# Splitting weights in pairs of rows and summing conditioning 1024 columns at a time, in a two-layer trunk on one Trainium2 core

## The chip, the cores and the metric

The kernel runs on one core of one Trainium2 chip (trn2). The metric is the device time of one execution in microseconds (us); the kernel before took 1552.6 us, the median of 3 runs (1552.41 to 1552.89).

## What is computed

Two layers of a conditioned decoder trunk over 256 tokens of width 1024, in fp32. Per layer, with the vector c of conditioning:

```python
mod = silu(c) @ ada_w[l] + ada_b[l]                  # 1024 x 6144
sh1, sc1, gt1, sh2, sc2, gt2 = split(mod, 6)
h = rms_norm(x, norm1_g[l]) * (1 + sc1) + sh1
proj = h @ w_in[l]                                   # 1024 x 3524
ya = retention(...); yb = forgetting_attention(...); yc = latent_attention(...)
g  = sigmoid(h @ gate_w + gate_b)                    # 1024 x 3072
x += gt1 * ((g0 * (ya @ br0) + g1 * (yb @ br1) + g2 * (yc @ br2)) @ out_w)
h = rms_norm(x, norm2_g[l]) * (1 + sc2) + sh2
x += gt2 * moe(h)                                    # 32 experts, top 2 of one group of 8
```

The two attentions are softmax attentions with 4 heads each, over blocks of 128 queries. A last RMSNorm follows the second layer.

## The kernel before, in words

**Stages.** The program runs mixer 0 (about 0 to 345 us of the trace), MoE 0 (to 790), mixer 1 (to 1077) and MoE 1 (to the end). All weights come from HBM through one ring of 12 slots of 1 MB (`SLOTS`, L58; the DMAs are issued on SP at L139), in one planned order. A slot is given back when its weights have been used, and the next transfer of the plan starts then. For a MoE the ring grows to 20 slots, in memory that the mixer has left: two on the right side and three in `ar` while the mixer still runs, three on the left (`open_extra(l, "left", 3)`, L1204) once its output projection is done.

**Rows of weights.** A mixer's products are made of "rows": 128 x 512 (or 128 x 452) weights against all tokens. For fp32 precision a row is split into a high and a low fp32r part, and each product takes three matmuls (`mm3`). `split_w` (L244) splits one row: ACT casts it into the high part (L253), DVE subtracts that from the weights (L255). There are four buffers `ws`. `pump` (L240) splits until three rows lie ready; `next_w` calls it before it hands a row to the matmuls, and `gemm_tok`, `gemm_feat` and `out` call it again behind each row's matmuls, before they yield. A layer has 144 rows.

**What else runs beside the rows.** At each yield the driver takes one step of every live generator: an attention (`softmax_head`, L652: scores on PE, bias and maximum on DVE, exponential on ACT at L664, after two more steps the normalising on DVE at L669, then the transposes on PE at L188 and their copy on ACT at L675), retention, and the conditioning chain. Instructions of an engine are issued in the order in which this interleaving writes them.

**Conditioning.** `ada` (L485) multiplies silu(c) into `ada_w`. Most of it is summed on DVE, since c is one vector: `acc` gets a 128 x 512 multiply (L509) and then 128 x 512 multiply-adds (L511), four to a 1 MB chunk of four row blocks of 512 columns, one per step; a 32-column matmul sums `acc` over partitions at the end. The result is read with one DVE add of the bias (L529) and, where sums lie in several partition groups, ACT copies (L531). At the start of the program the first four parts go over PE instead, straight from the slots, and `space` (before L1564) puts two `warm` matmuls (L190) behind each of the first four chunks; their result is not used. `gs` turns the sums into the scale and shift that the first `head` (L959) needs to form `hr`, the split activations, and no row can be multiplied before that.

**Out.** `out` (L1167) multiplies the last 16 rows; behind the last row of each half of the columns `residual` (L588) adds the result to x (L592, L593 on DVE, the squares on ACT at L594).

Of the kernel before, what the change touches and what calls it, by code (L numbers as in the profile page):

```python
# [17 lines left out]
P = 128  # L18
# [3 lines left out]
DEPTH = 2  # L22
# [35 lines left out]
SLOTS = 12  # L58
# [107 lines left out]
class Trunk:  # L166
# [73 lines left out]
    def pump(self):  # L240
        while self.stream and len(self.splits) < len(self.ws) - 1:
            self.split_w()

    def split_w(self):  # L244
# [11 lines left out]
        self.splits.append((hi, lo))  # L256
# [12 lines left out]
    def setup(self, pool, psum):  # L269
# [30 lines left out]
        self.adab = t("adab", [64, 512])  # L300
# [11 lines left out]
    def open_split(self, l):  # L312
# [3 lines left out]
        self.ws = [t(f"ws{i}", [P, 2, 512]) for i in range(4)]  # L316
# [40 lines left out]
    def plan_mixer(self, l):  # L357
# [4 lines left out]
        def put_ada(n):  # L362
            for _ in range(min(n, len(adas))):
                l_, m, h = adas.popleft()
                add((l_, "ada", m, h), rows(a["ada_w"][l_, m, h], 4), [P, 4, 512])

        def cols(name, w, c0, n, split=True, halves=(0, 1)):
            for h in halves:
                key = (l, name, c0, h)
                add(key, rows(w[h], 4), [P, 4, n])  # L370
                if split:
                    stream.extend((key, i, n, i == 3) for i in range(4))
                    put_ada(min(len(adas) - ADA_TAIL, spread.get((l, name, c0), 0)))

        adas = deque((l, m, h) for m in ((0, 2, 1, 3) if l == 0 else ()) + tuple(range(4, 12)) for h in range(2))
        if l + 1 < DEPTH:
            adas.extend((l + 1, m, h) for m in range(4) for h in range(2))
# [15 lines left out]
        for br in (2, 1, 0):  # L393
            for h in range(2):
# [3 lines left out]
                stream.extend((key, i, 512, i == 3) for i in range(4))  # L398
# [86 lines left out]
    def ada(self, l, m0, ms, space, R, vec=()):  # L485

        nc, ps = self.nc, self.S[3]
        full, begun = [], set()  # L490
# [6 lines left out]
        for m in ms:  # L497
            for h in range(2):
                key = (l, "ada", m0 + m, h)
                while vec and self.ring.behind(key) < (0 if self.hurry else ADA_LAG):  # L500
                    yield
                slot, v = self.ring.take(key)
                end = m == ms[-1] and h == 1
                if m in vec:
                    acc = self.acc[:, len(full)]
                    for t in range(4):
                        c = self.cz[:, 4 * h + t, 23:24]
                        if h == 0 and t == 0:
                            nc.vector.tensor_scalar(acc, v[:, t, :], c, None, ALU.mult)  # L509
                        else:  # L510
                            nc.vector.scalar_tensor_tensor(acc, v[:, t, :], c, acc, ALU.mult, ALU.add)  # L511
                        if t < 3:
                            yield from space(-1)
                    if h:
                        full.append(m)
                        if len(full) == 2 or m + 1 not in vec:
                            for _ in range(ADA_DELAY):
                                yield
                            for i, k in enumerate(full):
                                add_up(i, 8, k, self.acc[:, i], end)  # L520
                            full = []
                else:
                    for t in range(4):
                        add_up(t, 4 * h + t, m, v[:, t, :], end)
                self.ring.give(slot)
                yield from space(2 * m + h)
# [7 lines left out]
        return R[:n], all(m in vec for m in ms)  # L534

    def picks(self, rows, r, n=1):

        R, vec = rows
        if vec:
            return self.ident[:R.shape[0], r:r + 66].rearrange("p (q x) -> p q x", q=2)[:, :, 0:2 * n:2]  # L540
        return self.sel[:R.shape[0], r:r + 2 * n].rearrange("p (v q) -> p q v", q=2)

    def gs(self, l, i, r, rows, rows1=None):
# [4 lines left out]
        sv, R = self.picks(rows, r, 2), rows[0]  # L548
        R1 = rows1[0] if rows1 else R
# [25 lines left out]
    def gate_rows(self, r, off, rows, banks=None):  # L575

        self.gtb = self.v(off, D)
        sv, R = self.picks(rows, r), rows[0]
# [23 lines left out]
    def gemm_tok(self, n, evac, js=range(8), pa=None):  # L602

        pa = pa or [self.bank("g") for _ in range(NT)]
        for j in js:
# [5 lines left out]
            self.pump()  # L611
# [5 lines left out]
    def gemm_feat(self, acts, evac, js=None, pa=None):  # L617
# [3 lines left out]
        for j in js or range(nk):  # L621
# [8 lines left out]
            self.pump()  # L630
# [21 lines left out]
    def softmax_head(self, i, h, scores, bias, val, yr):  # L652
# [15 lines left out]
        for k, s in enumerate(parts):  # L668
            nc.vector.tensor_scalar(s, s, rs[:, k:k + 1], None, ALU.mult)  # L669
# [289 lines left out]
    def head(self, l):  # L959
# [43 lines left out]
        def split(n):  # L1003
            for _ in range(n):
                self.split_w()

# [13 lines left out]
        split(l)  # L1020
# [4 lines left out]
        split(l)  # L1025

    def mixer(self, l):
# [17 lines left out]
        def chain():  # L1045
            self.rowsA = yield from self.ada(l, 4, range(6), space, self.R, range(6))
# [7 lines left out]
            self.rowsB = yield from self.ada(l, 10, range(2), lambda i: later(i + 1), self.v(A_RB, 512),  # L1054
                                             range(min(2, inline // 2)))
            if l + 1 < DEPTH:
                rows = yield from self.ada(l + 1, 0, range(4), lambda i: later(i + 5 if i >= 0 else -1), self.acc[:, 1],
                                           range((inline - 4) // 2))
# [108 lines left out]
        def out():  # L1167
            pa = [[self.bank("g") for _ in range(NT)] for _ in range(2)]
            for h in range(2):
                for n in range(2):  # L1170
                    for j in range(4):
# [5 lines left out]
                        self.pump()  # L1177
# [26 lines left out]
        pool = self.open_extra(l, "left", 3)  # L1204
# [139 lines left out]
    def moe(self, l):  # L1344
# [51 lines left out]
        for p in range(NE // 2):  # L1396
# [28 lines left out]
            if p == 0:  # L1425
                R, vec = self.rowsB
                self.rowsB = self.acc[:R.shape[0], 1], vec
                nc.scalar.copy(self.rowsB[0], R)
# [212 lines left out]
```

## Time and profile before

| what | value |
|---|---|
| median of 3 runs | 1552.6 us |
| time of the profiled execution | 1548.41 us |
| its span, first to last instruction | 1546.7 us |
| PE / DVE / ACT busy, share of the span | 95% / 43% / 29% |
| moved by DMA | 535.16 MB, mean 346 GB/s |
| mean granted TensorE clock | 0.982 |

The profiled execution lies 4.2 us under the median of the runs, and 1.7 us of its time lie outside its span. Busy shares are means over stages that differ: in the MoEs PE and the DMA engines work all the time and DVE and ACT little; in the mixers DVE is busy up to the whole of a stretch.

### The profile page before, as it was taken

How to read it: one execution, taken by the hardware profiler on the slowest of the kernel's cores; microseconds unless marked ns; L12 is line 12 of the kernel's file. 1: busy time of each engine (PE TensorE's matmuls, PEld its weight loads, DVE VectorE, ACT ScalarE, POOL GpSimd, SP SyncE). 2: the span in 40 equal slices, each digit the busy share in tenths (PEclk: the TensorE clock that was granted, in tenths of full speed). 3: DMA queues.
4: the chain of work that ended last, by engine and by line, in shares of the span. 5: the costliest groups of instructions: out<-in, count | busy, mean ns of one | idle time of the engine just before them, and what ended most of it. 6: DMA issues, size and time to landing. Idle time of an engine off the chain costs nothing.

```text
span 1546.7 us, 21257 instructions
## 1 busy us (share of the span) xinstructions
PE 1471.0 (95%) x8326; PEld 901.9 (58%) x8326; DVE 662.7 (43%) x1756; ACT 451.4 (29%) x897; POOL 5.9 (0%) x10
## 2 busy tenths in 40 slices
PE   6898899999999999999979989999999999999996
PEld 3776889854444444444448779897444444444442
DVE  3766697951212222212157669767222222222223
ACT  3544544431111112111145554454211111111112
POOL 0000000000000000000000000000000000000001
PEclk9998999989999999999999999999999999999998
DMA  9963467989999999999995546667999999999993
GB/s 383 378 239 136 156 253 293 364 353 367 421 420 421 420 421 421 420 419 421 412 377 208 220 151 251 240 231 316 397 421 420 422 420 421 421 421 419 421 417 127
DMA packets 78542, 535.16 MB, mean 346 GB/s; under 512 B 8608, under 2 KB 8864, under 8 KB 15968
## 3 DMA queue, kind: packets, MB, share of 16 engines
q1 hardware_dynamic: 77776, 532.89, 85.3%
q8 instruction: 69, 1.13, 0.3%
q10 hardware_dynamic: 656, 0.80, 0.2%
q14 instruction: 41, 0.34, 0.1%
HBM read 532.61 MB, written 1.05 MB: 345 GB/s over the span
## 4 chain that ended last, share of the span: by engine, by line
PE 69%; DMA 15%; DVE 10%; ACT 4%; issue 2%; SPq 0%; DVEq 0%; ACTq 0%
PE bank L179 66%; DMA slot<-in_exp_w 6%; DMA more_left<-in_exp_w 3%; DVE ws L255 3%; DMA more_right<-in_exp_w 3%; PE bank L188 2%; DVE acc L511 2%; ACT ws L253 1%; DMA ar<-in_exp_w 1%; DMA slot<-in_w_in 1%; DMA slot<-in_ada_w 1%; ACT ar L664 1%; ACT ar L991 0%; ACT ar L1148 0%; DVE x L1392 0%
## 5 line engine op out<-in xcount | busy, mean ns | idle before, releaser
L179 PE MATMUL bank<-slot,ar 128*64 128x512 f32 (+1 forms) x1876 | 453.6, 593 | 1.0 <-ACT ar L1439 0.7
L179 PEld LDWEIGHTS bank<-slot,ar 128*64 128x64 f32 (+1 forms) x1876 | 143.0, 137 | 231.8 <-issue 214.7
L255 DVE TENSOR_TENSOR ws<-slot,ws 128x512 fp32r<-128x512 f32 (+1 forms) x276 | 187.5, 683 | 108.4 <-ACT ws L253 96.3
L179 PE MATMUL bank<-ar 128*64 128x512 f32 (+3 forms) x692 | 209.4, 502 | 4.3 <-DVE ar L887 3.1
L253 ACT CAST ws<-slot 128x512 fp32r<-128x512 f32 (+1 forms) x276 | 168.0, 618 | 141.1 <-PE bank L179 130.9
L179 PE MATMUL bank<-hr,ws 128*128 128x256 f32 x1536 | 202.4, 288 | 4.4 <-DVE ws L255 4.3
L179 PEld LDWEIGHTS bank<-hr,ws 128*128 128x128 f32 x1536 | 191.1, 193 | 13.5 <-DVE ws L255 5.4
L1341 ACT ACTIVATE ar<-bank,GS 128x128 f32<-128x128 f32 x128 | 58.6, 458 | 355.9 <-PE bank L179 325.2
L179 PE MATMUL bank<-ws,hr 128*128 128x512 f32 (+1 forms) x576 | 154.6, 415 | 7.2 <-ACT ws L253 3.4
L179 PE MATMUL bank<-more_left,ar 128*64 128x512 f32 x456 | 137.6, 594 | 0.0
L179 PEld LDWEIGHTS bank<-ar,x 128*128 128x128 f32 x1024 | 119.2, 192 | 25.1 <-issue 21.1
L179 PE MATMUL bank<-ar,x 128*128 128x128 f32 x1024 | 128.3, 278 | 1.8 <-DVE ar L1323 1.6
L179 PEld LDWEIGHTS bank<-ws,hr 128*128 128x128 f32 x576 | 109.4, 197 | 34.3 <-ACT ws L253 4.9
L179 PEld LDWEIGHTS bank<-ar 128*64 128x64 f32 (+2 forms) x692 | 81.4, 155 | 71.6 <-issue 59.3
L1458 DVE SCALAR_TENSOR_TENSOR yl<-bank,wsl,yh 128x512 fp32r<-128x512 f32 x60 | 45.0, 750 | 157.1 <-ACT yh L1457 157.1
L1375 DVE COPY wsl<-bank 64x1 f32<-64x1 f32 x64 | 10.0, 156 | 227.8 <-PE bank L179 227.4
L1339 DVE TENSOR_SCALAR ar<-bank,GS 128x128 f32<-128x128 f32 x128 | 52.4, 410 | 116.4 <-ACT ar L1341 116.4
L1422 DVE TENSOR_TENSOR R<-R,bank 128x512 f32<-128x512 f32 x32 | 22.0, 688 | 177.8 <-PE bank L179 177.8
L511 DVE SCALAR_TENSOR_TENSOR acc<-slot,cz,acc 128x512 f32<-128x512 f32 x122 | 90.8, 744 | 0.1
L179 PEld LDWEIGHTS bank<-more_left,ar 128*64 128x64 f32 x456 | 41.0, 137 | 82.5 <-issue 76.3
L1457 ACT ACTIVATE yh<-bank,wsl 128x512 fp32r<-128x512 f32 x60 | 41.2, 687 | 150.7 <-PE bank L179 150.7
L1418 ACT ACTIVATE R<-bank 128x512 f32<-128x512 f32 x32 | 19.2, 599 | 198.0 <-PE bank L179 198.0
(244 smaller groups left out, 1221.5 us busy)
## 6 DMA issues: line engine op xcount, KB each, us to landing
slot<-in_exp_w SPq DMA_DIRECT2D x226, 1024.0 KB, 19.8
ar<-in_exp_w SPq DMA_DIRECT2D x54, 1024.0 KB, 19.8
more_left<-in_exp_w SPq DMA_DIRECT2D x54, 1024.0 KB, 19.8
slot<-in_ada_w SPq DMA_DIRECT2D x46, 1024.0 KB, 6.8
more_right<-in_exp_w SPq DMA_DIRECT2D x38, 1024.0 KB, 19.3
slot<-in_w_in SPq DMA_DIRECT2D x24, 1024.0 KB, 10.4
slot<-in_gate_w SPq DMA_DIRECT2D x23, 1024.0 KB, 5.0
slot<-in_branch_w SPq DMA_DIRECT2D x12, 1024.0 KB, 4.8
```

Source lines behind the costliest of these rows:

```text
L179: self.nc.tensor.matmul(out, lhsT, rhs, start=start, stop=stop, skip_group_check=True)
L188: self.nc.tensor.transpose(out, in_, self.ident[:n, :n])
L253: self.nc.scalar.copy(hi, w)
L255: self.nc.vector.tensor_tensor(lo, w, hi.bitcast(F32), ALU.subtract)
L511: nc.vector.scalar_tensor_tensor(acc, v[:, t, :], c, acc, ALU.mult, ALU.add)
L664: nc.scalar.activation(s, s, AF.Exp, bias=nm[:, k:k + 1], accum_out=sm[:, k:k + 1])
L1339: nc.vector.tensor_scalar(hgT[:, j], pv[:, i], G[:, j:j + 1], S[:, j:j + 1], ALU.mult, ALU.add)
L1341: nc.scalar.activation(hgT[:, j], pv[:, i], AF.Identity, bias=S[:, j:j + 1], scale=G[:, j:j + 1])
L1418: nc.scalar.activation(hid, G[0], AF.Silu)
L1422: nc.vector.tensor_tensor(hid, hid, G[1], ALU.mult)
L1457: nc.scalar.mul(self.yp[n][0], G[n], wsl(p))
L1458: nc.vector.scalar_tensor_tensor(self.yp[n][1], G[n], wsl(p), self.yp[n][0].bitcast(F32), ALU.mult, ALU.subtract)
```

## The change

`split_w` takes two rows at a time: ws has three buffers of two rows, ACT and DVE each issue one 128 x 1024 instruction for a pair. `pump` gives out two of the three buffers ahead and is called in `next_w` alone, so a split stands in the engines' order behind the steps of the live generators. The ring has 11 slots; it grows by four instead of three on the left for the MoE. The conditioning chunks hold two row blocks of 1024 columns, and DVE sums 1024 columns at a time; the bias is added by one DVE instruction over all partition groups, and the ACT copies go. The parts at the start are still multiplied on PE (`ada_start`), with one pair of warm matmuls instead of four. `softmax_head` normalises on ACT. The first split of the program stands before the first head's scaling, and the MoE's end splits one pair instead of two rows. The core of the diff:

```diff
-SLOTS = 12
+SLOTS = 11
     def pump(self):
-        while self.stream and len(self.splits) < len(self.ws) - 1:
+        while self.stream and (len(self.splits) + 1) // 2 < len(self.ws) - 1:
             self.split_w()
     def split_w(self):
-        w = self.held[key][1][:, i, :n]
+        w = self.held[key][1][:, i:i + 2, :n]
         t = self.ws[self.wsi % len(self.ws)]
-        hi, lo = t[:, 0, :n], t[:, 1, :n]
+        hi, lo = t[:, 0, :, :n], t[:, 1, :, :n]
         self.nc.scalar.copy(hi, w)
         self.nc.vector.tensor_tensor(lo, w, hi.bitcast(F32), ALU.subtract)
-        self.splits.append((hi, lo))
+        self.splits.extend((hi[:, k], lo[:, k]) for k in range(2))
...
-        self.ws = [t(f"ws{i}", [P, 2, 512]) for i in range(4)]
+        self.ws = [t(f"ws{i}", [P, 2, 2, 512]) for i in range(3)]
...
+    def ada_start(self, ms, space, R):
+        ps = self.S[3]
+        for m in ms:
+            for h in range(2):
+                slot, v = self.ring.take((0, "ada", m, h))
+                for t in range(4):
+                    self.mm(ps[32 * t:32 * t + 32, :], self.cz[:, 4 * h + t, 23 - m:55 - m], v[:, t, :],
+                            m == ms[0] and h == 0, m == ms[-1] and h == 1)
+                self.ring.give(slot)
+                yield from space(2 * m + h)
+        self.nc.vector.tensor_tensor(R, ps, self.adab, ALU.add)
+        yield
...
+                if k < vec:
+                    for t in range(2):
+                        c = self.cz[:, 2 * q + t, 23:24]
+                        if q + t == 0:
+                            nc.vector.tensor_scalar(acc, v[:, t], c, None, ALU.mult)
+                        else:
+                            nc.vector.scalar_tensor_tensor(acc, v[:, t], c, acc, ALU.mult, ALU.add)
+                        if t == 0:
+                            yield from space(-1)
...
         n = 32 * len(begun)
-        b = 64 if all(m in vec for m in ms) else 32
-        nc.vector.tensor_tensor(R[:b], ps[:b], self.adab[:b], ALU.add)
-        while b < n:
-            nc.scalar.copy(R[b:2 * b], ps[b:2 * b])
-            b *= 2
+        nc.vector.tensor_tensor(R[:n], ps[:n], self.adab[:n], ALU.add)
...
@@ gemm_tok, gemm_feat, out
-            self.pump()
             yield
@@ softmax_head
-            nc.vector.tensor_scalar(s, s, rs[:, k:k + 1], None, ALU.mult)
+            nc.scalar.mul(s, s, rs[:, k:k + 1])
...
-        pool = self.open_extra(l, "left", 3)
+        pool = self.open_extra(l, "left", 4)
...
             def space(i):
+                if i == 0:
+                    self.warm(2)
                 if i == 1:
                     next(head)
-                self.warm(2)
                 return ()
...
             next(gs)
+            self.split_w()
             next(head)
```

On PE, at the start of the program before (`cst` of 128x224 is a warm matmul, `slot,cz` a conditioning chunk, `cst,R` the reading of its sums, `hr` and `ws` the first row):

```order
L188 MATMUL bank_68<-cst,ar 128x128 x4
L179 MATMUL bank_69<-cst 128x224 x2
L179 MATMUL bank_70<-slot_91,cz 32x512 x4
L179 MATMUL bank_69<-cst 128x224 x2
L179 MATMUL bank_70<-slot_92,cz 32x512 x4
L179 MATMUL bank_69<-cst 128x224 x2
L179 MATMUL bank_69<-cst,R 128x2 x4
L179 MATMUL bank_65<-ws_0_135,hr_0_139 128x452 x3
```

And the same place with the change:

```order
L188 MATMUL bank_68<-cst,ar 128x128 x4
L179 MATMUL bank_70<-slot_91,cz 32x512 x4
L179 MATMUL bank_70<-slot_92,cz 32x512 x4
L179 MATMUL bank_69<-cst,R 128x2 x4
L179 MATMUL bank_65<-ws_0_133,hr_0_136 128x452 x3
```

Three pairs of warm matmuls are gone from between the chunks; the pair behind the first chunk stays.

On DVE, behind the in-projection of mixer 0 (about 67 us of the trace), where conditioning (L511, then L529) stands between the splits (L255); before:

```order
L255 TENSOR_TENSOR ws_0_135<-slot_93,ws_0_135 128x512
L511 SCALAR_TENSOR_TENSOR acc<-slot_95,cz,acc 128x512
L255 TENSOR_TENSOR ws_0_136<-slot_93,ws_0_136 128x512
L511 SCALAR_TENSOR_TENSOR acc<-slot_95,cz,acc 128x512
L255 TENSOR_TENSOR ws_0_137<-slot_93,ws_0_137 128x512
L511 SCALAR_TENSOR_TENSOR acc<-slot_95,cz,acc 128x512
L825 COPY lfx<-bank_69 128x8
L255 TENSOR_TENSOR ws_0_138<-slot_93,ws_0_138 128x512
L509 TENSOR_SCALAR acc<-slot_94,cz 128x512
```

And with the change:

```order
L255 TENSOR_TENSOR ws_0_133<-slot_92,ws_0_133 128x1024
L529 SCALAR_TENSOR_TENSOR acc<-slot_97,cz,acc 128x1024
L729 TENSOR_SCALAR ar<-ar,sm 128x256
L730 TENSOR_SCALAR ar<-ar,sm 128x128
L729 TENSOR_SCALAR ar<-ar,sm 128x256
L730 TENSOR_SCALAR ar<-ar,sm 128x128
L529 SCALAR_TENSOR_TENSOR acc<-slot_97,cz,acc 128x1024
L255 TENSOR_TENSOR ws_0_134<-slot_95,ws_0_134 128x1024
L529 SCALAR_TENSOR_TENSOR acc<-slot_99,cz,acc 128x1024 x2
L832 COPY lfx<-bank_69 128x8
L255 TENSOR_TENSOR ws_0_135<-slot_95,ws_0_135 128x1024
```

Before, one 512-column sum stood behind each split of one row; now two 1024-column sums stand between two splits of a pair.

On ACT, at the first two softmax heads of mixer 0 (L664 is the exponential before, L671 now; L676 the normalising, which was on DVE; L675 and L682 the copy of the transposes; L253 the casts); before:

```order
L664 ACTIVATE ar,sm<-ar,sm 128x128
L664 ACTIVATE ar,sm<-ar,sm 128x256
L253 CAST ws_0_135<-slot_92 128x512
L664 ACTIVATE ar,sm<-ar,sm 128x128
L664 ACTIVATE ar,sm<-ar,sm 128x256
L253 CAST ws_0_136<-slot_92 128x512
L253 CAST ws_0_137<-slot_92 128x512
L675 COPY ar<-bank_68 128x384
L253 CAST ws_0_138<-slot_92 128x512
L675 COPY ar<-bank_69 128x384
```

And with the change:

```order
L671 ACTIVATE ar,sm<-ar,sm 128x128
L671 ACTIVATE ar,sm<-ar,sm 128x256
L671 ACTIVATE ar,sm<-ar,sm 128x128
L671 ACTIVATE ar,sm<-ar,sm 128x256
L253 CAST ws_0_133<-slot_96 128x1024
L676 ACTIVATE ar<-ar,sm 128x128
L676 ACTIVATE ar<-ar,sm 128x256
L682 COPY ar<-bank_68 128x384
L676 ACTIVATE ar<-ar,sm 128x128
L676 ACTIVATE ar<-ar,sm 128x256
L253 CAST ws_0_134<-slot_96 128x1024
L682 COPY ar<-bank_69 128x384
```

The two heads' exponentials now follow each other without a cast between them, the normalising stands behind a cast of a pair, and the second head's normalising stands behind the copy of the first head's transposes.

## Rows read from the trace of the kernel before

**Rows 1.** The page, busy time of the engines: us (share of the span) xinstructions.

```profile
PE 1471.0 (95%) x8326; PEld 901.9 (58%) x8326; DVE 662.7 (43%) x1756; ACT 451.4 (29%) x897; POOL 5.9 (0%) x10
```

**Rows 2.** The page, chain that ended last, share of the span by engine.

```profile
PE 69%; DMA 15%; DVE 10%; ACT 4%; issue 2%; SPq 0%; DVEq 0%; ACTq 0%
```

**Rows 3.** Windows: stretch, length, busy us (instructions) by engine, TensorE's clock, DMA share, GB/s.

```profile
60.00:77.00 17.00, 15.19 (x122) 14.65 (x122) 16.25 (x52) 9.83 (x19) 0.00 (x0) 1.00 0.84 323
...
180.00:220.00 40.00, 38.07 (x307) 35.66 (x306) 38.83 (x98) 16.32 (x30) 0.00 (x0) 1.00 0.68 249
...
260.00:300.00 40.00, 39.90 (x286) 36.84 (x286) 38.90 (x65) 21.89 (x40) 0.00 (x0) 1.00 0.91 350
...
385.00:790.00 405.00, 401.90 (x2083) 184.32 (x2083) 87.71 (x253) 65.21 (x123) 0.00 (x0) 1.00 1.01 419
...
940.00:980.00 40.00, 38.36 (x309) 35.92 (x308) 38.87 (x104) 16.96 (x31) 0.00 (x0) 1.00 0.67 250
```

**Rows 4.** Groups by line and form: xcount | busy us, mean ns of one | idle before.

```profile
L255 DVE TENSOR_TENSOR ws<-slot,ws 128x512 fp32r<-128x512 f32 x260 | 178.1, 687 | 101.5 <-ACT ws L253 91.5 <-PE bank L179 7.6 <-DMA slot<-in_gate_w 0.3
L253 ACT CAST ws<-slot 128x512 fp32r<-128x512 f32 x260 | 159.7, 621 | 137.5 <-PE bank L179 127.4 <-DVE ws L255 3.8 <-DVE acc L511 3.1
L511 DVE SCALAR_TENSOR_TENSOR acc<-slot,cz,acc 128x512 f32<-128x512 f32 x122 | 90.8, 744 | 0.1
L255 DVE TENSOR_TENSOR ws<-slot,ws 128x452 fp32r<-128x452 f32 x16 | 9.4, 624 | 6.8 <-ACT ws L253 4.8 <-DMA slot<-in_w_in 1.9
L253 ACT CAST ws<-slot 128x452 fp32r<-128x452 f32 x16 | 8.3, 566 | 3.5 <-PE bank L179 3.5
L669 DVE TENSOR_SCALAR ar<-ar,sm 128x256 f32<-128x256 f32 x16 | 5.6, 347 | 0.0
```

**Rows 5.** DVE's timeline behind the in-projection of mixer 0.

```profile
62.48 0.69 DVE L255 TENSOR_TENSOR ws<-slot,ws 128x512 fp32r<-128x512 f32 x1
63.09 0.75 DVE L511 SCALAR_TENSOR_TENSOR acc<-slot,cz,acc 128x512 f32<-128x512 f32 x1
63.75 0.16 DVE L212 TENSOR_TENSOR sm<-sm 128x4 f32<-128x4 f32 x1
```

**Rows 6.** Start of mixer 0, timeline: start us, us, what [idle before <-releaser].

```profile
18.99 1.02 PE L179 MATMUL bank<-cst 128*128 128x224 f32 x4
...
21.79 1.17 ACT L531 COPY R<-bank 32x512 f32<-32x512 f32 x2 [4.85 <-DVE R L529]
...
26.88 1.50 ACT L253 CAST ws<-slot 128x452 fp32r<-128x452 f32 x3
...
27.50 0.75 PE L179 MATMUL bank<-ws,hr 128*128 128x452 f32 x1 [3.43 <-ACT ws L253]
```

**Rows 7.** The softmax's normalising (L669): who waited for it, us and times.

```profile
  PE bank L188: 18.4, 9
```

**Rows 8.** Windows of L255 alone: stretch, length, DVE busy us (xcount), clock, DMA.

```profile
180.00:220.00 40.00, 14.72 (x22) 1.00 0.68 249
...
260.00:300.00 40.00, 17.85 (x28) 1.00 0.91 350
```

**Rows 9.** End of mixer 0's output projection, timeline.

```profile
313.30 3.90 DVE L511 SCALAR_TENSOR_TENSOR acc<-slot,cz,acc 128x512 f32<-128x512 f32 x5
...
317.11 0.68 DVE L592 TENSOR_TENSOR ar<-bank,ar 128x512 f32<-128x512 f32 x1
```

**Rows 10.** End of mixer 1's output projection, timeline.

```profile
1065.19 0.69 DVE L255 TENSOR_TENSOR ws<-ar,ws 128x512 fp32r<-128x512 f32 x1 [1.30 <-ACT ws L253]
```

**Rows 11.** A window ahead of MoE 1's first pairs.

```profile
1080.00:1100.00 20.00, 18.76 (x107) 8.90 (x106) 5.66 (x20) 5.43 (x10) 0.00 (x0) 1.00 0.95 386
```

**Rows 12.** The same of L511 alone.

```profile
180.00:220.00 40.00, 11.88 (x16) 1.00 0.68 249
```

**Rows 13.** Chain of waits in the middle of MoE 1: start us, us, what.

```profile
1322.75 19.84 DMA slot<-in_exp_w
```

**Rows 14.** A window of 2 us at the first rows of mixer 0, columns as rows 3.

```profile
30.00:32.00 2.00, 2.00 (x7) 1.72 (x7) 0.69 (x1) 0.62 (x1) 0.00 (x0) 0.50 1.00 416
```

More of the change, by code (lines that the diff above doesn't have):

```diff
@@ L364, in put_ada @@
                 l_, m, h = adas.popleft()
-                add((l_, "ada", m, h), rows(a["ada_w"][l_, m, h], 4), [P, 4, 512])
+                if l_ == 0 and m < 4:
+                    add((l_, "ada", m, h), rows(a["ada_w"][l_, m, h], 4), [P, 4, 512])
+                else:
+                    add((l_, "ada", m, h), rows(a["ada_w"][l_, m + h // 2, h % 2], 2), [P, 2, 1024])
         def cols(name, w, c0, n, split=True, halves=(0, 1)):
@@ L397, in plan_mixer @@
                 add(key, rows(a["branch_w"][l, br, h], 4), [P, 4, 512])
[L398 removed]
+                stream.extend((key, i, 512, i == 2) for i in (0, 2))
                 if br < 2:
@@ L495, in add_up @@
             begun.add(i)
[L497 to L500, printed above, removed]
+        for p in range(pairs):
+            for q in range(4):
+                key = (l, "ada", m0 + 2 * p, q)
+                while self.ring.behind(key) < (0 if self.hurry else ADA_LAG):
                     yield
                 slot, v = self.ring.take(key)
[L503 to L509, printed above, removed]
-                        else:
-                            nc.vector.scalar_tensor_tensor(acc, v[:, t, :], c, acc, ALU.mult, ALU.add)
-                        if t < 3:
+                end = p == pairs - 1 and q == 3
+                if k < vec:
[3 more added lines that the diff above has]
+                            nc.vector.tensor_scalar(acc, v[:, t], c, None, ALU.mult)
+                        else:
+                            nc.vector.scalar_tensor_tensor(acc, v[:, t], c, acc, ALU.mult, ALU.add)
+                        if t == 0:
@@ L513, in ada @@
                             yield from space(-1)
[L514 to L521, printed above, removed]
-                else:
-                    for t in range(4):
-                        add_up(t, 4 * h + t, m, v[:, t, :], end)
+                    if q == 3 or k == vec - 1:
+                        for _ in range(ADA_DELAY):
+                            yield
+                        for i in range(2):
+                            add_up(i, 8, 2 * p + i, acc[:, 512 * i:512 * i + 512], end)
+                else:
+                    for t in range(2):
+                        for i in range(2):
+                            add_up(2 * t + i, 2 * q + t, 2 * p + i, v[:, t, 512 * i:512 * i + 512], end)
@@ L525, in ada @@
                 self.ring.give(slot)
-                yield from space(2 * m + h)
+                yield from space(k)
+                k += 1
         n = 32 * len(begun)
-        b = 64 if all(m in vec for m in ms) else 32
-        nc.vector.tensor_tensor(R[:b], ps[:b], self.adab[:b], ALU.add)
-        while b < n:
-            nc.scalar.copy(R[b:2 * b], ps[b:2 * b])
-            b *= 2
-        yield
[L534 to L540, printed above, removed]
+        nc.vector.tensor_tensor(R[:n], ps[:n], self.adab[:n], ALU.add)
@@ L541, in picks, with gs @@
+        yield
+        return R[:n]
+    def picks(self, R, r, n=1):
         return self.sel[:R.shape[0], r:r + 2 * n].rearrange("p (v q) -> p q v", q=2)
-    def gs(self, l, i, r, rows, rows1=None):
+    def gs(self, l, i, r, R, R1=None):
         nc = self.nc
@@ L573, in router_terms, with gate_rows @@
         yield
-    def gate_rows(self, r, off, rows, banks=None):
+    def gate_rows(self, r, off, R, banks=None):
         self.gtb = self.v(off, D)
-        sv, R = self.picks(rows, r), rows[0]
+        sv = self.picks(R, r)
         for n in range(2):
@@ L1019, in head @@
         high(2)
-        split(l)
+        if l:
+            self.split_w()
         scaled(3)
@@ L1024, in head @@
         low(3)
-        split(l)
+        if l:
+            self.split_w()
     def mixer(self, l):
@@ L1045, in chain @@
         def chain():
-            self.rowsA = yield from self.ada(l, 4, range(6), space, self.R, range(6))
+            self.rowsA = yield from self.ada(l, 4, 3, space, self.R, 12)
             yield from self.gs(l, 1, 12 * l + 6, self.rowsA)
```

52 lines of the change are left out of this document (23 added, 29 removed).

## Prediction

> **What bounds the kernel now.** I read the page's busy shares first: PE works 95% of the span [rows 1], so a change can win only what PE does not do, or does late. The chain of waits says whom PE waits for: 69% of the span runs over PE, 15% over DMA, 10% over DVE, 4% over ACT [rows 2]. The windows by stretch then say where. In MoE 0 (385 to 790) PE is busy 401.90 of 405 us while the DMA engines move 419 GB/s at a share of 1.01; DVE and ACT are nearly idle there, so nothing of what this change does to them counts in a MoE. In the mixers DVE is the engine that fills up: 38.83 of 40 us in 180 to 220, 38.90 in 260 to 300, 38.87 in 940 to 980, 16.25 of 17 in 60 to 77 [rows 3]. The change acts on the mixers, some 630 of 1547 us, and in them on the places where PE waits for DVE or ACT; what it saves elsewhere lies beside matmuls.
>
> **What the new instructions cost.** None of 1024 columns is in the trace. Two widths are: from 452 to 512 columns a split on DVE goes from 624 to 687 ns, 1.05 ns a column, and a cast on ACT from 566 to 621, 0.92 a column [rows 4]. Straight lines give 1.22 us for a DVE split of a pair, 1.09 for its cast and, with DVE's slope, 1.28 for a sum of conditioning (744 ns at 512). Against two of the old by their durations that saves 0.15, 0.15 and 0.21 us. But on a full DVE starts count, not durations: a split at 62.48 is followed by the next instruction 0.61 us later, a sum at 63.09 by the next 0.66 later [rows 5]. By starts a pair costs 2 x 0.61 = 1.22 now and 1.22 less the same overlap of 0.08, about 1.14, then: 0.08 saved. I take 0.08; 0.15 and 0 are its ends. [...]
>
> **Part by part.**
>
> Start of mixer 0: -3.6. No row can be multiplied before the first scale and shift. On that path stood warm matmuls behind the second and third chunk, each about a microsecond (1.02 at 18.99); the pair behind the fourth lies beside the DVE add. Two pairs go: -1.9. The two ACT copies at L531 (1.17) go: -1.2. The first row waits for a cast of 0.5 us behind the casts of hr (PE stands 3.43 us until 27.50) [rows 6]; that split now stands ahead: -0.5. Ends: -5, and -1.5 if the third and fourth chunk land no earlier than they are multiplied now.
>
> Conditioning in 60 to 77: +1.5. Behind the in-projection the order puts two sums between two splits, where one of half the width stood behind each split. Over eight rows DVE issues seven and a half sums of 1.2 us (by starts) where it had eight of 0.66, about 4 us more, in a stretch with 16.25 of 17 us busy and 15.19 us of PE work [rows 3]. Ends 0 (two pairs ready ahead are a cushion) and +3.
>
> Softmax heads: +1.0. Normalising (347 ns and a shorter one per head, [rows 4]) moves to ACT. PE waits 18.4 us, nine times, for it now [rows 7], so this is on the path. DVE is freed, and splits no longer stand between a head's steps; but a cast of a pair, 1.09 us where one of 0.62 stood, now stands ahead of the first head's normalising, and the second head's stands behind the first head's copy, which waits for PE. Ends -3 and +3, a sixth of the wait each way.
>
> Full stretches 180 to 220 and 260 to 300: -1.5. 22 and 28 rows are split there [rows 8], 25 pairs of 0.08 make -2; the sums come denser and take back 0.5. Ends -4 (by durations) and +3 (denser sums, as in 60 to 77).
>
> Mixer 1, 940 to 1005: -4. The order has the conditioning that `gs` and the gates of layer 1 wait for done some eight rows earlier; about three chunks, twelve sums of 0.66 us, leave the rows of this stretch, whose first 40 us are full of DVE work [rows 3], for the rows ahead of it or vanish in wider sums. Of these 8 us I take half, since PE itself works 38.36 of those 40. Ends -7 and 0.
>
> Tails of the output projections: +1.0. In mixer 0 five sums of 3.90 us stand ahead of the last residual, which starts at 317.11 [rows 9]; they go, but the last pair's cast and split are longer and stand behind the first residual: -1. In mixer 1 no sums stand there; the last row is split at 1065.19 [rows 10]. Now the last two rows wait for one pair behind the residual's squares; the pair's split starts and ends about half a microsecond later each, and two rows of 1.4 us (39.90 us of PE for the 28 rows of [rows 3, 8]) follow it where one did: +2. Ends 0 and +2.
>
> Ring: +1.0. One slot less until the left side grows means that 1 MB more, 2.5 us at 420 GB/s, has to be moved after 1066. In 1080 to 1100 the DMA share is 0.95, one microsecond spare [rows 11]. Ends 0 and 2.5.
>
> At nothing I cost the cheaper splits beside matmuls (if that cover went, 144 pairs of 0.08 us would give 11 us), the bias add over 128 partitions (one instruction of the same 512 columns), and the second half of w_in, which is issued one slot later and needed some 20 us after.
>
> Sum: -3.6 + 1.5 + 1.0 - 1.5 - 4 + 1.0 + 1.0 = -4.6. The profiled execution took 1548.41, 4.2 below the median; its own forecast is 1543.8, that of the median **1548.0**.
>
> **Rivals.**
>
> *The sums in bunches stall the rows: slower.* DVE issues in order, and a split behind two sums of 1.28 us is late once both pairs ahead are used up; a pair lasts PE 2.8 us, so it decides where DVE's work for a pair exceeds that. For: DVE is full in three stretches already. Against: two pairs ahead are more than three rows. Price: sums take about 12 us of a full stretch [rows 12]; in half the rows they add 6, of which PE's idle time there (1.9 of 40 us in 180 to 220, [rows 3]) gives back at most 1.9: +4.1 in mixer 0 for the -1.5, +3 for 60 to 77, and 0 for the -4 in mixer 1. The sum, -3.6 + 3 + 1 + 4.1 + 0 + 1 + 1, is +6.5: **1559.1**; with half the price in mixer 0 about 1557.
>
> *The MoEs swallow it: no measurable change.* In the middle of MoE 1 the chain goes over transfers, from 1322.75 on [rows 13], and in MoE 0 the DMA share is 1.01 [rows 3]. If the transfers, not PE's arrival, set the end, an earlier PE only waits longer. Against: in mixer 1 the DMA engines are at 0.67 [rows 3], so the ring is full there and the first transfers start when slots come free, earlier by as much. The mixers' terms sum to -5.6; half of that lost is about **1551**, all of it 1553.6.
>
> [...]
>
> *Everything that is DVE-bound shrinks: a larger gain.* With starts spaced by the full 0.15 saved, the heads at -3 and mixer 1 at -7 the sum is about -12: **1540.5**.
>
> **How the numbers follow.** A difference under 0.2%, 3.1 us, cannot be told from none. The forecast's case (1544 to 1549.5) has 0.36, the larger gain 0.11, the two cases of no change together 0.28, the slower one 0.25. That gives 0.47 faster, 0.28 same, 0.25 slower. The terms' ends, taken as independent, spread by about 6 us either way; the range reaches down past the larger gain's centre to 1540 and up to the half-priced rival, to 1558, which leaves out a tenth on each side.
>
> **What would show it.** First row on PE near 24 us rather than 27.50; no ACT copy behind the bias add; one DVE split of a pair at about 1.22 us; the last row of 60 to 77's block one or two microseconds later; PE's wait for the normalising near 18.4 us, now for ACT; DVE below full at 960 to 1000; the last residual of mixer 1 at two microseconds more behind its first half than now. The forecast is wrong if PE's waits for splits (ws) grow by more than 5 us, or if MoE 1 grows longer by what the mixers win.

## The result, and the profile after

The changed kernel takes **1569.57 us** (median of 4 runs, 1568.96 to 1570.89) against 1552.51 of the kernel before in the same call: a ratio of **1.0128**, 95% interval 1.0108 to 1.0147. It is 17 us slower, outside the range of the prediction and on the other side. The profiled execution has a span of 1567.3 us, 20.6 more than before.

The page of the kernel after, its busy engines and its chain, against [rows 1, 2]:

```profile
PE 1473.7 (94%) x8318; PEld 899.9 (57%) x8318; DVE 631.0 (40%) x1508; ACT 434.9 (28%) x777; POOL 5.9 (0%) x10
...
PE 39%; DMA 8%; DVE 5%; ACT 2%; issue 1%; DVEq 0%; ACTq 0%; SPq 0%
```

DVE did 32 us less and ACT 16 us less, as the change means it, and PE 2.7 us more. So the engines' work does not explain the loss; waits do. (The chain's shares sum to little more than half: followed back from the end of the program it breaks off at 683 us, behind the wait in MoE 0 below.)

Where the time went is read from three marks that both programs have on PE: the first row of a mixer (`ws,hr`), and the small product `cst,sm` at the start of a MoE. Timeline of PE before (start us, us, what, [idle before <-releaser]):

```profile
356.04 0.19 PE L179 MATMUL bank<-cst,sm 128*1 128x1 f32 x2 [1.25 <-DVE sm L1357]
...
801.22 4.58 PE L179 MATMUL bank<-ws,hr 128*128 128x452 f32 x19 [0.62 <-ACT hr L998]
...
1097.45 0.19 PE L179 MATMUL bank<-cst,sm 128*1 128x1 f32 x2 [1.24 <-DVE sm L1357]
```

And after:

```profile
23.23 6.67 PE L179 MATMUL bank<-ws,hr 128*128 128x452 f32 x24 [3.30 <-ACT hr L1005]
...
356.53 0.19 PE L179 MATMUL bank<-cst,sm 128*1 128x1 f32 x2 [1.25 <-DVE sm L1359]
...
810.56 1.76 PE L179 MATMUL bank<-ws,hr 128*128 128x452 f32 x5 [0.40 <-ACT hr L1005]
...
1116.38 0.19 PE L179 MATMUL bank<-cst,sm 128*1 128x1 f32 x2 [1.25 <-DVE sm L1359]
```

| stretch | before, us | after, us | difference |
|---|---|---|---|
| to the first row (27.50 in [rows 6]) | 27.5 | 23.2 | -4.3 |
| mixer 0, first row to its MoE's mark | 328.5 | 333.3 | +4.8 |
| MoE 0, mark to the first row of mixer 1 | 445.2 | 454.0 | +8.8 |
| mixer 1, the same | 296.2 | 305.8 | +9.6 |
| MoE 1, mark to the end | 449.3 | 450.9 | +1.6 |

The start won what was forecast. Both mixers lost, and so did MoE 0, in which the change touches little more than the first slots.

**The mixers.** What PE waited for in the first 345 us (in total, times, longest), before:

```profile
PE bank L188 <- DVE ar L669: 10.9, 4, 4.1
...
PE bank L179 <- DVE ws L255: 2.7, 3, 1.8
```

and after:

```profile
PE bank L179 <- DVE ws L255: 14.3, 13, 3.9
...
PE bank L188 <- ACT ar L676: 7.9, 5, 3.7
```

The wait for the normalising shrank; that for splits (`ws`) grew from 2.7 to 14.3 us. The longest is the place of [rows 5]. PE there, after:

```profile
57.21 3.13 PE L179 MATMUL bank<-hr,ws 128*128 128x256 f32 x24 [1.02 <-DVE ws L255]
64.19 4.07 PE L179 MATMUL bank<-hr,ws 128*128 128x256 f32 x20 [3.85 <-DVE ws L255]
```

and DVE there, after:

```profile
57.08 1.28 DVE L529 SCALAR_TENSOR_TENSOR acc<-slot,cz,acc 128x1024 f32<-128x1024 f32 x1
...
58.95 1.28 DVE L529 SCALAR_TENSOR_TENSOR acc<-slot,cz,acc 128x1024 f32<-128x1024 f32 x1
...
62.91 1.23 DVE L255 TENSOR_TENSOR ws<-slot,ws 128x1024 fp32r<-128x1024 f32 x1
64.06 1.28 DVE L529 SCALAR_TENSOR_TENSOR acc<-slot,cz,acc 128x1024 f32<-128x1024 f32 x1
```

Between 57.08 and 62.91 DVE had two sums and 24 small instructions of the live generators' steps to do, all ahead of the split that PE stood for. Before, splits stood among them at 60.53 and 62.48 (the latter in [rows 5]). PE stood 3.85 us, and then ran at a granted clock of 0.50, the lower of the two values, 0.50 and 1.00, that the clock takes in the traces of before and after (the columns of this window are length, PE busy, clock, DMA share, GB/s):

```profile
64.00:66.00 2.00, 1.81 (x8) 0.50 1.03 430
```

**MoE 0.** At its middle every engine jumps over a block that handles overflowing experts. The records of that jump on PE's queue (L1485 before, L1486 after; min/median/max ns of the two MoEs), before:

```profile
L1485 PEldq COMPARE_BRANCH  x2: 445/454/462, 676.1 to 1418.4; - x2
```

after:

```profile
L1486 PEldq COMPARE_BRANCH  x2: 461/3219/5977, 676.8 to 1437.3; - x2
```

In MoE 1 it takes 0.46 us as before, in MoE 0 it takes 5.98. PE stands, and comes back at half the clock (windows of the kernel after; columns as [rows 3]):

```profile
676.00:683.00 7.00, 0.96 (x3) 0.49 (x3) 0.23 (x2) 0.00 (x0) 0.00 (x0) 0.91 1.01 415
683.00:687.00 4.00, 3.89 (x10) 1.38 (x12) 0.69 (x4) 0.00 (x0) 0.00 (x0) 0.50 1.02 420
```

The DMA queues show what goes with a slow jump. Queue 8, of kind `instruction`, moves 69 packets of 16 KB in either program; away from the jumps one comes for every 250 or so of PE's instructions, in mixers and MoEs alike, so the packets are taken here to hold PE's own instructions. In the 21 us ahead of the jump (655 to 676) the kernel before has one (packets, MB, share of 16 engines):

```profile
q1 hardware_dynamic: 1211, 8.83, 101.1%
q8 instruction: 1, 0.02, 0.3%
```

The changed kernel has none from 655 to the start of the jump at 676.8 (the first line is all that there is of that window), and one in the 6 us of the jump, 676.8 to 682.8 (the second):

```profile
q1 hardware_dynamic: 1262, 9.19, 101.4%
...
q8 instruction: 1, 0.02, 1.1%
```

**The new instructions** cost what was forecast: a pair's split 1.22 us, its cast 1.05, a sum 1.28 (groups by form, as [rows 4]):

```profile
L255 DVE TENSOR_TENSOR ws<-slot,ws 128x1024 fp32r<-128x1024 f32 x132 | 160.5, 1221 | 128.4 <-ACT ws L253 128.2
L253 ACT CAST ws<-slot 128x1024 fp32r<-128x1024 f32 x132 | 136.6, 1050 | 63.4 <-PE bank L179 57.3 <-DMA slot<-in_ada_w 2.5 <-ACT ws L253 1.8
L529 DVE SCALAR_TENSOR_TENSOR acc<-slot,cz,acc 128x1024 f32<-128x1024 f32 x61 | 78.0, 1279 | 0.4
```

The split at 62.91 us above is followed by the next instruction 1.15 us later.

### The profile page after: what moved, and what is told of

Read it like the earlier page. It is cut to its first block, busy times and chain, and to the rows that moved or that the text cites. A ratio compares the mean times of both kernels' runs of the same rounds, so it can differ in the third digit from the quotient of the medians.

```text
span 1567.3 us, 20679 instructions
## 1 busy us (share of the span) xinstructions
PE 1473.7 (94%) x8318; PEld 899.9 (57%) x8318; DVE 631.0 (40%) x1508; ACT 434.9 (28%) x777; POOL 5.9 (0%) x10
## 3 DMA queue, kind: packets, MB, share of 16 engines
HBM read 532.74 MB, written 1.05 MB: 341 GB/s over the span
## 4 chain that ended last, share of the span: by engine, by line
PE 39%; DMA 8%; DVE 5%; ACT 2%; issue 1%; DVEq 0%; ACTq 0%; SPq 0%
PE bank L179 38%; DMA slot<-in_exp_w 3%; DMA ar<-in_exp_w 2%; DMA more_left<-in_exp_w 1%; DMA more_right<-in_exp_w 1%; DVE ws L255 1%; PE bank L188 1%; DVE acc L529 1%; ACT ws L253 1%; DMA slot<-in_w_in 0%; ACT ar L671 0%; ACT ar L676 0%; DVE x L1394 0%; DVE R L1393 0%; DVE sm L670 0%
## 5 line engine op out<-in xcount | busy, mean ns | idle before, releaser
L179 PE MATMUL bank<-slot,ar 128*64 128x512 f32 (+2 forms) x1728 | 493.7, 600 | 7.8 <-PEq L1486 5.9
L179 PEld LDWEIGHTS bank<-slot,ar 128*64 128x64 f32 (+1 forms) x1728 | 152.0, 139 | 221.6 <-issue 207.4
L179 PE MATMUL bank<-ar 128*64 128x512 f32 (+3 forms) x696 | 246.9, 504 | 1.5 <-DVE ar L894 0.9
L255 DVE TENSOR_TENSOR ws<-slot,ws 128x1024 fp32r<-128x1024 f32 (+1 forms) x140 | 169.0, 1214 | 131.4 <-ACT ws L253 131.1
L179 PE MATMUL bank<-more_left,ar 128*64 128x512 f32 x608 | 203.7, 595 | 0.0
L253 ACT CAST ws<-slot 128x1024 fp32r<-128x1024 f32 (+1 forms) x140 | 143.9, 1044 | 72.6 <-PE bank L179 57.3
L179 PEld LDWEIGHTS bank<-ar 128*64 128x64 f32 (+2 forms) x696 | 92.2, 156 | 90.6 <-issue 76.1
L179 PE MATMUL bank<-more_right,ar 128*64 128x512 f32 x304 | 137.2, 595 | 0.2 <-DVE yl L1460 0.2
L179 PEld LDWEIGHTS bank<-more_left,ar 128*64 128x64 f32 x608 | 60.3, 137 | 82.5 <-issue 76.0
L179 PE MATMUL bank<-yr,ws 128*128 128x256 f32 x576 | 77.0, 287 | 4.3 <-DVE ws L255 3.5
```

Of the source, the lines that this page charges most:

```text
L179: self.nc.tensor.matmul(out, lhsT, rhs, start=start, stop=stop, skip_group_check=True)
L253: self.nc.scalar.copy(hi, w)
L255: self.nc.vector.tensor_tensor(lo, w, hi.bitcast(F32), ALU.subtract)
```

## The experiments

The theories: **B**, sums of twice the width at the same pace per step are twice as dense and hold up the splits; **L**, the splits are late because they stand behind the live generators' step; **N**, the normalising is worse on ACT; **S**, the ring's lost slot; **J**, a jump that is slow or fast by its place in PE's instructions; **P**, two warm pairs at the start lie on the path to the first row; **C**, warm matmuls hold the clock up. Ratios are to the kernel before in the same call, with 95% intervals; "mixer 0" and "mixer 1" are the lengths of the table above in the profiled execution (before: 328.5 and 296.2; after: 333.3 and 305.8).

**e1_paced** undoes the density alone:

```diff
                         if t == 0:
                             yield from space(-1)
+                            yield from space(-1)
...
                 self.ring.give(slot)
+                if k < vec:
+                    yield from space(-1)
                 yield from space(k)
```

> The changed kernel, but each 1024-column sum of conditioning now takes two steps of the chain instead of one, so that it goes as fast by columns as before the change. Theory B (the sums come twice as dense and hold up the splits on DVE): the rows after the in-projections (+5.6 us in mixer 0, +5.0 in mixer 1) and the rows behind the attentions (+9 in 175 to 270, +5 in 895 to 1015) come back, 12 us or more: about 1557. Theory L (the splits are late because they stand behind the attention's step): PE still waits some 14 us for ws in mixer 0, 1566 or more. Theory S (one slot less and later transfers): no change, 1569.

1557.82 us, ratio 1.0051 (1.0031 to 1.0070); mixer 0 325.1, mixer 1 303.1. B holds: without the density the changed kernel is 12 us faster. PE still waits 8.6 us for ws in mixer 0, so it is not all.

**e2_pump** undoes the place of the splits alone:

```diff
+            self.pump()
             yield
```

(in gemm_tok, gemm_feat and out)

> The changed kernel with the call of pump put back in front of each yield, so that a pair is split ahead of the attention's step once a buffer is free; the dense sums stay. Theory L: PE's waits for ws in mixer 0 fall from 14.3 us to under 5, and the time by about 10, to 1560. Theory B: the same DVE work in the same rows only changes its order, the rows of 56 to 78 and 190 to 210 stay within 2 us of now: 1567 to 1570.

1559.94 us, ratio 1.0063 (1.0044 to 1.0082); mixer 0 330.8, mixer 1 299.3. L holds as well, at 10 us; the waits for ws in mixer 0 fall to 5.2 us.

**e3_both** has both edits.

> Both together: sums at the old pace and pump in front of the yield. If B and L are the whole loss, the mixers are as fast as before the change or faster by the 4 us of the start: 1549 to 1554. If one of them is nothing, this equals the run of the other one alone. If MoE 0 keeps its 3 us and mixer 1 its tail, 1555.

1538.56 us, ratio **0.9919** (0.9897 to 0.9941): 31 us less than the changed kernel, where the two alone gave 12 and 10; mixer 0 317.2, mixer 1 292.3. It beat every forecast: the two losses hide each other. With either of them left PE still stands for splits in the first 345 us, 8.6 us with late splits (e1_paced) and 5.2 with dense sums (e2_pump); with neither the waits for ws are all but gone:

```profile
PE bank L179 <- DVE ws L255: 1.5, 1, 1.5
```

**e4_norm** puts the normalising back on DVE in the changed kernel, **e5_norm_dve** in e3_both:

```diff
-            nc.scalar.mul(s, s, rs[:, k:k + 1])
+            nc.vector.tensor_scalar(s, s, rs[:, k:k + 1], None, ALU.mult)
```

> The changed kernel with the softmax normalised on DVE again. Theory N (the normalising on ACT, behind a pair's cast, holds up the transposes): PE's waits for it, 7.9 us in mixer 0, fall, and the time by 4: 1565. Theories B and L: DVE gets 7 us more work in each mixer where it is full already: 1570 to 1574.

1566.47 us, ratio 1.0106 (1.0085 to 1.0127): its interval overlaps that of the changed kernel, so it is unclear there. Its mixer 0 is as long as the changed kernel's (333.5), its mixer 1 is 3 us shorter (302.6).

> Sums at the old pace, pump in front of the yield, and the softmax normalised on DVE as before the change. Theory N (on ACT it stands behind a pair's cast and is late): PE's 8.1 us of waits for it in mixer 0 fall by half, 3 to 5 us less than with both alone, a ratio of 0.989 to the kernel before. The other theory (DVE is the fuller engine): 7 us more work on DVE in each mixer, a third of it on the path: 0.995.

1530.51 us, ratio 0.9878 (0.9855 to 0.9900) against 0.9919; mixer 0 313.1 and mixer 1 286.2, 4 and 6 us shorter. The intervals touch, but both mixers' lengths point to N: with DVE relieved of the rest, the normalising is better off there. These lengths are of one profiled execution each.

**e6_before_late** is the kernel before without the three calls of pump ahead of a yield:

```diff
-            self.pump()
             yield
```

> The kernel before, single rows and 512-column sums, with nothing changed but that pump is called in next_w alone, so that each split stands behind the step of the live generators. Theory L (the place of the split costs by itself): PE waits for ws in the rows after the in-projections and in the tails, 5 to 10 us slower, ratio 1.003 to 1.006. If the place only hurts where pairs and dense sums are in the way: within 2 us, ratio 1.000.

1548.96 us, ratio 0.9991 (0.9977 to 1.0005); mixer 0 327.4, mixer 1 297.6. For single rows the place of the split costs nothing that the time shows, though PE's waits for ws in the first 345 us grow from 2.7 to 7.2: L is not a cost of its own.

**e7_before_dense** is the kernel before with the old 512-column sums at twice the pace:

```diff
-                        if t < 3:
+                        if t == 1:
                             yield from space(-1)
```

> The kernel before with two of its 512-column sums issued in one step of the chain, so that the conditioning goes twice as fast by columns; single rows, pump in front of the yield. Theory B (density by itself): the rows after the in-projection and behind the attentions grow as in the changed kernel, 6 to 12 us slower, ratio 1.004 to 1.008. If density only hurts where the splits are late too: within 3 us, ratio 1.000 to 1.002.

1578.76 us, ratio **1.0187** (1.0165 to 1.0209); mixer 0 341.2, mixer 1 310.7, 12.7 and 14.5 us longer, twice the dearer forecast. Density costs by itself, with single rows and early splits.

**e12_pairs** is the kernel before with pairs alone: the diff above of `SLOTS`, `pump`'s condition, `split_w`, `ws`, the stream in pairs, and the fourth slot on the left; pump still ahead of each yield.

> The kernel before with the splits in pairs alone (three buffers of two rows, 11 slots, four on the left), pump in front of the yield, 512-column sums, warm matmuls and normalising as before. If wider splits are what gains: 3 to 6 us faster, ratio 0.996 to 0.998. If the pairs come late or the slot is missed: 1.001 to 1.004.

1533.92 us, ratio **0.9912** (0.9885 to 0.9940); mixer 0 317.1, mixer 1 290.9. Pairs alone win 14 us, more than twice the forecast, and the lost slot (S) is not to be seen: its MoEs take 445.5 and 449.2 us.

**e15_pairs_late** takes from e12_pairs the three calls of pump that e6_before_late takes from the kernel before.

> The kernel before with the splits in pairs (0.9912 with pump in front of the yield) and pump in next_w alone; 512-column sums at their old pace, all warm matmuls. If a late pair hurts by itself: PE waits for ws after the in-projections and in the tails, 8 to 14 us slower than with pump in front, ratio 0.997 to 1.000. If late splits hurt only together with the dense sums (single rows lost nothing by it, 0.9991): within 2 us of 0.9912.

1557.10 us, ratio 1.0060 (1.0037 to 1.0082), 23 us more than with early pairs and dearer than either forecast; mixer 0 330.2, mixer 1 302.5. Waits in the first 345 us of e12_pairs:

```profile
PE bank L179 <- ACT ws L253: 3.8, 1, 3.8
...
PE bank L179 <- DVE ws L255: 2.3, 3, 1.7
```

and of e15_pairs_late:

```profile
PE bank L179 <- DVE ws L255: 11.4, 14, 2.8
...
PE bank L179 <- ACT ws L253: 6.2, 4, 3.8
```

So a late pair is costly without any dense sum, where a late single row is not. In `next_w` a single row is split when two lie ready, in every step; a pair is split when two rows lie ready, every second step, and takes a cast of 1.05 and a split of 1.22 us in a row, 2.3 us against 1.3, behind a whole step's work.

**e8_warm** is e3_both with all four warm pairs, **e10_after_warm** the changed kernel with them:

```diff
             def space(i):
-                if i == 0:
-                    self.warm(2)
                 if i == 1:
                     next(head)
+                self.warm(2)
                 return ()
```

> Sums at the old pace and pump in front of the yield, with all four pairs of warm matmuls at the start put back. Theory P (two pairs lie on the path): the first row starts 1.9 us later and the run is 2 us slower than with both alone, ratio 0.9931. Theory C (the clock): warm matmuls keep the clock up for the first rows, 2 us faster than with both alone, ratio 0.9906.

1531.61 us, ratio 0.9883 (0.9861 to 0.9904) against 0.9919: faster, though the first row starts at 24.83 instead of 23.78. The gain is not at the start. MoE 0 took 445.5 us instead of 454.1, and the jump 0.45 instead of 6.16. The intervals touch; the two stretches are plain.

> The changed kernel with nothing undone but the three pairs of warm matmuls at the start. Theory J (24 instructions more on PE move the jump over MoE 0's overflow block away from the place at which it takes 5.9 us): the jump takes 0.45 us again, the first row starts 1 us later, and the run is 4 to 6 us faster than the changed kernel, ratio 1.009 to 1.010. Theory P (the pairs lie on the path): 1 to 2 us slower, 1.014.

1563.50 us, ratio 1.0095 (1.0066 to 1.0123); the jump takes 0.45 us, MoE 0 445.8.

**e11_before_nowarm** is the kernel before with that diff the other way round, and nothing else.

> The kernel before without the second to fourth pair of warm matmuls, nothing else. Theory J: the jump's place on PE moves 24 instructions ahead, to where the slow ones are, and takes 5.9 us; with 1.9 us won at the start the run is 3 to 5 us slower, ratio 1.002 to 1.003. Theory P: the jump stays at 0.45 us and the run is 2 us faster, ratio 0.9988. Theory C (the clock): the first rows run longer at half the clock, 2 us slower, with the jump at 0.45.

1563.14 us, ratio 1.0116 (1.0074 to 1.0158), well above what theory J gave. The first row starts 1.6 us earlier, at 25.9, mixer 0 is 4.3 us shorter and mixer 1 1.6 longer (324.2 and 297.8), and now *both* jumps are slow:

```profile
L1485 PEldq COMPARE_BRANCH  x2: 6088/6109/6130, 670.2 to 1421.9; - x2
...
676.58 5.93 PE L179 MATMUL bank<-more_right,ar 128*64 128x512 f32 x16 [6.04 <-PEq L1485]
...
1428.38 8.94 PE L179 MATMUL bank<-slot,ar 128*64 128x512 f32 x32 [5.90 <-PEq L1485]
```

MoE 0 takes 453.1 and MoE 1 457.1 us, 8 more each, where one slow jump had been expected.

**e14_after_fill** is the changed kernel with six matmuls elsewhere, in the gap in which PE waits for the first activations; **e13_fill** has them in e5_norm_dve:

```diff
             next(gs)
+            for _ in range(6):
+                self.mm(self.S[3][:, 0:C_U], self.ident, self.cst[:, 0:C_U], True, True)
             self.split_w()
```

> The changed kernel with nothing but those six matmuls in the gap at the start. Theory J: the jump takes 0.45 us and the run is 5 to 8 us faster than the changed kernel, ratio 1.0075 to 1.0095. If the jump is only slow by what the DMA queues hold at that moment: 5.9 us again, ratio 1.012 to 1.013.

1559.84 us, ratio 1.0080 (1.0054 to 1.0105); the jump takes 0.44 us, MoE 0 445.9. Between the chunks or behind them, the same matmuls make the jump fast. J is shown: by the trace's records the jump of MoE 0 stands behind 7344 to 7350 of PE's instructions in the seven programs where it takes some 6 us, and behind 7367 to 7374 in the others; the one long jump of MoE 1 behind 15611, the short jumps there behind 15621 to 15649. It is not the time at which PE arrives: e2_pump jumps at 674.2 us and is slow, e6_before_late at 674.5 and is fast. The packets of queue 8 divide the 34 jumps of the 17 programs in the same way: ahead of each of the 26 short jumps one starts 3.2 to 5.5 us before the jump; ahead of the 8 long jumps none does in the last 24.8 us, the next starts 3.4 to 3.7 us into the jump, takes 1.1, and the jump ends 1.4 us after that.

> Sums at the old pace, pump in front of the yield, normalising on DVE, one pair of warm matmuls as in the changed kernel, and six matmuls of the same kind in the 3.3 us in which PE waits for the first activations. Theory J (the jump's place): 24 instructions more on PE, the jump takes 0.45 us in MoE 0; theory P: the first row starts at 23.5, not 25.7; theory C: the matmuls in the gap keep the clock up for the first rows, 1 to 2 us. All three: ratio 0.981 to 0.984. If the position does not matter and only warm matmuls between the chunks do: 0.988 with a jump of 5.9 us.

1521.07 us, ratio **0.9824** (0.9791 to 0.9857): the fastest version. The first row starts at 24.3 and now at the full clock, 1.00 granted, where the changed kernel, e11 and the kernel before [rows 14] have 0.50:

```profile
24.00:26.00 2.00, 1.62 (x7) 1.00 1.01 422
26.00:28.00 2.00, 2.00 (x11) 1.00 1.02 426
```

The changed kernel, in the first of these windows:

```profile
24.00:26.00 2.00, 2.00 (x6) 0.50 1.01 422
```

**e9_best**, e5_norm_dve with all four warm pairs, joins the gains found before e13_fill:

> Sums at the old pace, pump in front of the yield, normalising on DVE, and all four pairs of warm matmuls: if the gains of the last two add up on top of the 0.9919 of the first two (0.9878 and 0.9883, so -0.0041 and -0.0036), the ratio to the kernel before is 0.984, about 1528 us.

1525.06 us, ratio 0.9850 (0.9822 to 0.9879): the gains add up to within 0.001 of the forecast ratio, some 1.5 us, and the matmuls in the gap are 4 us better still, though the intervals overlap.

## Why the prediction was wrong

*Start, -3.6:* right; -4.3 measured in this stretch. The warm pairs were on the path, with 1.6 us of it (e11_before_nowarm); how the rest divides between the ACT copies and the earlier split no run tells.

*What the new instructions cost:* right to 0.04 us, and by starts a pair takes 1.15 us where two single rows take 1.22, 0.07 saved for the 0.08.

*Full stretches, -1.5, "25 pairs of 0.08":* this step mis-sized pairs. Alone they won 14 us (e12_pairs). The sum counted what DVE saves in its full stretches and put the rest at nothing, as hidden beside matmuls; its own price for the case that this cover went, 11 us, was the nearer one. Both mixers got shorter, 0 by 11 us and 1 by 5. Of the 11, 5.4 lie behind row 136, where the kernel before runs at a granted clock of 0.54 (320 to 330 us, under the tails below), so a part of the gain is the clock's. By which of their savings (DVE's, ACT's, or fewer turns between them) pairs win the rest no run tells apart.

*The place of the splits:* this is the step that failed. The prediction had pump's move only as a gain ("splits no longer stand between a head's steps") and as a cushion ("two pairs ready ahead are a cushion"), and gave the wait that it adds no price. It cost 23 us with pairs (e12_pairs to e15_pairs_late); in the changed kernel 10 with the dense sums (e2_pump) and 19 without them (e1_paced to e3_both). The prediction's own sign of being wrong came with it: PE's waits for ws grew by more than 5 us, in mixer 0 from 2.7 to 14.3. Two pairs are ahead only just after a split; when the next one is issued, two rows are left, 2.8 us of PE (39.90 for the 28 rows of [rows 3, 8]), for a step's work and 2.3 us of cast and split.

*Conditioning in 60 to 77, +1.5, and the rival of bunched sums:* the mechanism was right and the size was not. The rows of that block took 22.3 us instead of 16.7 (row starts on PE), +5.6; rows 8 to 15 of mixer 1, the like place there, which was not costed, +5.0; rows 64 to 111 of mixer 0, +9.4 for the -1.5. In the changed kernel density cost 12 us (e1_paced), in the kernel before 26 (e7_before_dense). What was not in the price is the clock: behind the stand of 3.85 us the rows show 0.50 (64 to 66 us).

*Mixer 1, 940 to 1005, -4:* the conditioning did end earlier, but the rows ahead of it paid for it: the 48 rows around (48 to 95) took 4.7 us more. Its condition, that PE can use the time, was the one that bunching took away.

*Softmax heads, +1.0:* in the changed kernel 3 us, at its end and not clear of the noise (e4_norm); with the other two losses gone +10 over both mixers (e3_both to e5_norm_dve, from single profiles), beyond its end.

*Tails, +1.0:* mixer 1 as forecast. In mixer 0 the part from row 136 (counted from 0) to the MoE's mark got 5.5 us shorter, not 1. No sums stand in it any more, but that is not shown to be the reason: e12_pairs keeps five sums ahead of its last residual and is 5.4 us shorter there too, and e6_before_late, with single rows, 3.8. What the runs show instead is the clock behind the last rows. The kernel before, then e12_pairs at the like place (columns as at the stand above):

```profile
320.00:330.00 10.00, 10.00 (x51) 0.54 1.01 424
...
310.00:320.00 10.00, 8.68 (x70) 1.00 0.99 401
```

The changed kernel and e6_before_late have 1.00 in 320 to 330.

*Ring, +1.0, and the MoEs that swallow:* MoE lengths do not depend on the mixers: 445.0 to 445.9 and 449.2 to 450.9 us in all runs with a fast jump, whether the mixers were 25 us shorter or 27 longer. That rival is out, and the lost slot cost nothing that shows: MoE 1 takes 449.2 us in e12_pairs, which has 11 slots, and 449.3 before.

*A clock that takes back what the start wins, one of the two cases of no change:* not at the start. The rows of the changed kernel run at 0.50 in 24 to 26 us, 0.89 in 26 to 28 and 1.00 in 28 to 34; the kernel before, whose first row starts 4.3 us later, shows 0.50 from 26 to 32 ([rows 14] are the last 2 us of it) and 0.94 in 32 to 34. Elsewhere the changed kernel's rows show 0.50 behind the stands of 3.85 us in mixer 0 (64 to 66) and 3.86 us in mixer 1 (836 to 838) and behind the slow jump of 5.98 (683 to 687). At the start 0.50 stands behind PE's gap with all four pairs ahead of it as well, in the kernel before (3.43 us, [rows 6]) and in e9_best (0.50 from 26 to 28 us); with matmuls in the gap itself, in e13_fill, the rows show 1.00 from 24 to 28.

*Not thought of:* the jump. Removing six matmuls at the start cost 8.8 us 650 us later. The bill by runs, from the kernel before: pairs -14, the start -4, the jump 8.8; of the 17 us this leaves some 26 for late pairs, dense sums and the normalising on ACT together, which hide one another and are not split further.

## What to carry to other kernels

Where an engine issues in order, ask of a wider instruction not what it saves but what now stands ahead of the instruction that the bottleneck waits for: pairs of rows split ahead of the step won 14 us here (e12_pairs), the same pairs behind it took 23 us more than that (e15_pairs_late). When a stream of background work is made wider, halve its pace per step with it: here that was worth 12 us (e1_paced). And compare the lengths of stages that an edit does not touch: a shift of 8 us in one of them was the place of a jump and no effect of the edit's idea.

## What the runs showed of the hardware that was not expected

The jump of PE over a block that is not executed took 0.44 to 0.46 us in some programs and 5.92 to 6.16 in others, and 24 instructions more or fewer ahead of it, between the first chunks or in the gap behind them, switched it; on ACT and DVE the same jump took 45 to 72 ns in the kernel before, the changed one and e11_before_nowarm. With the time at half the clock behind it (0.50 in 683 to 687 us of the changed kernel) a slow one costs 6 to 11 us: MoE 0 takes 453.1 to 455.8 us with it and 445.0 to 445.9 without, MoE 1 457.1 and 449.2 to 450.9. In those 6 us a packet of 16 KB of kind `instruction` comes in on queue 8, which in every program with a fast jump had come ahead of it. That PE stands for its own instructions is the reading that fits all 34 jumps; no row names what the packet holds, and no run moves the jump's target by itself.

With six matmuls in the stand of 3.3 us ahead of the first rows the granted clock was 1.00 in 24 to 26 us (e13_fill, e14_after_fill); with that stand empty it was 0.50 there (the changed kernel).
